# A two-layer fp32 network on one core: the recurrent layer's output projection as seven block products, plain rows at the start of the second MLP, and the first means further back

## The chip, the cores and the metric

The kernel runs on one core of one Trainium2 chip. The metric is the device time of one execution in microseconds (us). Three runs of the kernel before gave 2066.32, 2066.69 and 2067.29 us; the median is **2066.69 us**. PE is TensorE's matrix multiplication, PEld its weight load, DVE is VectorE, ACT ScalarE, POOL GpSimd, SP SyncE, which issues nearly all DMAs.

## What is computed

Two layers over 1024 tokens of 1024 features, all in fp32: layer 0 mixes tokens with a sliding-window attention, layer 1 with a gated recurrence; each is followed by an MLP, and a norm ends it. Cut to what matters here:

```python
def hgrn2_recurrence(h, lower_bound, w_in, g_norm, w_o):
    q, f, i, g = jnp.split(h @ w_in, 4, axis=-1)
    ...                                   # chunked gated recurrence, 8 heads of 128
    o = rmsnorm(o, g_norm) * jax.nn.silu(g.astype(jnp.float32))
    return o.astype(h.dtype) @ w_o        # 1024 x 1024: the output projection

def sqrelu_mlp(h, w_up, w_down):
    return jnp.square(jax.nn.relu(h @ w_up)) @ w_down

def reference(x, ...):
    for layer in range(2):
        h = rmsnorm(x, mix_norm[layer])
        y = attention(h, ...) if layer == 0 else hgrn2_recurrence(h, ...)
        x = x + y
        x = x + sqrelu_mlp(rmsnorm(x, mlp_norm[layer]), w_up[layer], w_down[layer])
    return rmsnorm(x, final_norm)
```

## The kernel before

**Tiles.** Activations lie transposed, features on the 128 partitions and tokens along the row: the residual stream is 8 feature tiles (`kt`) by 2 token halves (`hf`) of 128 x 512. Every fp32 operand is split into a high part (a cast to fp32r, mostly on ACT) and a low part (the difference, mostly on DVE); `split` (L523) does it for activations, `weight_split` (L505) for weights. A block product is then three matmuls, high by high, high by low, low by high (`mm3`, L487), each with 128x128 weights and a row of 512, or of 256 in the inner products. In a row of the profile `wh` and `wl` are split weights, `wr` a raw weight, `a` and `t` long- and short-lived tiles, `m` a few more, `sm` small ones, `d` DRAM, and `p` and `q` PSUM banks, four of each. Every operation is issued by one helper, so the line is L429 nearly everywhere.

**Order of work.** The program is first recorded as a list of operations in the order in which the code is written. A list scheduler (`Schedule`, L156) then lays each engine's queue out, with modelled costs, by the rank of an operation: its place in the list minus a `lead` that the code may set (`LEAD`, 100 places, for weights; `EVACUATE` for what reads a `p` bank). Nothing is reordered at run time: each engine goes through its queue, and an instruction that waits holds up all behind it on its engine.

**First means.** `scaled` (L589) makes the attention's input x times gain, split, and sums the squares over the 8 feature tiles on ACT and DVE. `token_rstd` (L546) then multiplies that sum by a constant column on PE (8 matmuls of one column) to get each token's mean and makes its normaliser.

**Recurrence and its output projection.** `hgrn` (L1631) runs 8 heads; head e+1's gates (projections) are interleaved with head e's `recurrence` (L1458), which ends with the head's gated output `g` for each half, split in two. `hgrn_out` (L1607), called once for each half, is a plain product: for each of 8 output blocks m one `p` bank gets 8 block products, is multiplied by the normaliser `r` and added to x. Between the two halves, `mlp_first` (L681) makes the second MLP's first operands: x times gain, split (`begin`, L631), and with `weigh(0)` (L625) the means of half 0, which also writes that half of x to DRAM.

**MLPs.** `mlp` (L918) computes the up product by a Strassen scheme of seven products over (feature halves) x (token halves), one pair of output rows at a time: `pair(m)` (L819) for m = 0 to 15. Products 1 and 2 of the rows 0 and 1 are begun early (`pair_first`, L805, called by `mlp_second`, L686). From row pair 2 on (`leaves`) the products 2, 3 and 4 aren't multiplied in full: two row pairs together compute each by a second Strassen level (`inner_products`, L779), seven quarter products with rows of 256, whose sums DVE adds up. `inner_operands` (L732) makes their operands. `weigh(1)` comes before the pairs.

The functions that the change touches, and what calls them:

Of the kernel before, what the change touches and what calls it, by code (L numbers as in the profile page):

```python
# [14 lines left out]
ALU = mybir.AluOpType  # L15
AX = mybir.AxisListType

P = 128
T = 1024
D = 1024  # L20
KT = D // P
NH = 2
TH = T // NH
# [351 lines left out]
class Net:  # L375
# [38 lines left out]
    def a(self, dt=F32, shape=(P, TH)):  # L414
        return self.tile("a", BUFS["a"], shape, dt)
# [185 lines left out]
    def square_relu(self, m, hf, c, psum):  # L601
# [79 lines left out]
    def mlp_first(self, layer):  # L681
        self.layer, self.hid, self.y = layer, {}, {}
        yield from self.begin(2 + layer)
        self.weigh(0)

    def mlp_second(self):  # L686
        self.first = [self.pair_first(m) for m in range(2)]
# [131 lines left out]
    def pair(self, m, x, leaves):  # L819
# [5 lines left out]
        up, half = self.io["up"][self.layer], MT // 2  # L825
        last, odd = m == half - 1, m % 2
        inner, four = [], ("12", "56", "73", "4")
        if leaves and odd:
            inner.append((2, (up[m - 1][:, TH:], 2), four, (1, 3, 5, 7)))
# [3 lines left out]
        elif leaves and m > 3:  # L833
            inner.append((4, (up[m - 2 + half][:, TH:], up[m - 1 + half][:, TH:]), four, (1, 3, 5, 7)))
            inner.append((3, (), four[2:], (2, 5)))
        w = self.strassen_weights(up[m], up[m + half], (2, 3, 4) if leaves else (1, 2), inner)

        def read(ps):
            z = self.t()
            self.copy(z, ps)  # L840
            return z
# [4 lines left out]
        def between(k):  # L846
            for z in now[k]:
                next(z)

        main, side = self.psum("q") if leaves else self.first[m], self.psum("q")  # L850
        now = [()] * 4
        if leaves:
            self.product(main, w[1], x[1], True)
            u1 = read(main)
            self.sums[2].append((m, u1))
            if odd:
                z2 = leaf(2, ((1, 2), (6, 5), (7, 3), (4,)))
                now = [[z2], [z2], [z2], [z2]]
            elif m > 3:
                z4, z3 = leaf(4, ((1, 2), (6, 5), (7, 3), (4,))), self.rest  # L860
                z3.send(w)
                now = [[z4, z3], [z4, z3], [z4], [z4]]
        between(0)
        self.product(side, w[5], x[5], True)
        p5 = read(side)
# [33 lines left out]
        if odd:  # L899
            for n, u in self.sums[2][-2:]:  # L900
                self.square_relu(n, 0, u, False)
        elif m > 3:
# [15 lines left out]
    def mlp(self, cut):  # L918

        x = self.mlp_second()  # L920
        for m in range(MT // 2):
            if m == 2:
# [535 lines left out]
    def recurrence(self, e, gates, totals, out):  # L1458
# [80 lines left out]
        for hf, (q, k) in enumerate(zip(qs, ks)):  # L1539
# [32 lines left out]
                totals.append(self.a())  # L1572
                self.ts("Pool", totals[hf], sq, 1.0, None, ALU.mult)
            self.stt(g, o, self.gain(5, e), g, ALU.mult, ALU.mult)
            keep = e < KT - 1
            y = self.split(g, self.t if keep else None)
            out[hf].append(self.put_by(y) if keep else y)
            yield

    def back(self, kept):  # L1580
# [23 lines left out]
            self.tt("DVE", new[hf], tv[:, :, 0], tv[:, :, 1], ALU.mult, n)  # L1604
        return at + n, new, *out

    def hgrn_out(self, hf, y, total):  # L1607
        r = self.t()
        self.copy(r, self.rstd(total, 0.25, 0.25))
        for m in range(KT):  # L1610
            w = self.blocks(self.weight(self.io["wg"][m]))
            x = self.t()
            self.dma(x, self.x[m][hf], 4 * P * TH)
            ps = self.psum()
            for kt in range(KT):
                self.mm3(ps, w[kt], y[kt], kt == 0, kt == KT - 1)
            z = self.t()
            self.tt("DVE", z, ps, r, ALU.mult)
            self.x[m][hf] = self.a()
            self.tt("any", self.x[m][hf], x, z, ALU.add)  # L1620

    def spill(self, hf):
        for kt in range(KT):
# [7 lines left out]
    def hgrn(self, layer):  # L1631
        self.hgrn_constants()
        x, r = self.finish(layer, True), [self.a() for _ in range(NH)]
        begun = [self.two_first(which, 0, x) for which in ((0, 3), (1, 2))]
        self.rs.append(self.token_rstd(self.sum_squares([self.x[kt][1] for kt in range(KT)]), keep=True))
        for y, z in zip(r, self.rs):
            self.copy(y, self.spread(z))
        self.spill(1)
        ys, totals = [[], []], []
        before = iter(())  # L1640
        for e in range(KT):
            got = []
            interleave(self.gates(e, x, self.rs, r, got, [None] * 2 if e else begun), before, 14, 13)
            before = self.recurrence(e, got, totals, ys)
# [31 lines left out]
def run(pieces):  # L1676
    for _ in pieces:
        pass
# [22 lines left out]
def layout(i):  # L1701
# [23 lines left out]
        "wg": f(i["hgrn_w_o"][0].reshape(KT, P, KT, P).transpose(2, 1, 0, 3).reshape(KT, P, D)),  # L1725
# [40 lines left out]
```

## Time and profile before

| | before |
|---|---|
| median of three runs | 2066.69 us |
| the profiled execution's own time | 2068.61 us |
| its span, first to last instruction | 2066.8 us |
| PE, matmuls | 2057.5 us busy, 12248 matmuls |
| DVE | 1831.0 us busy |
| ACT | 1203.6 us busy |
| DMA | 407.43 MB, mean 197 GB/s |
| granted TensorE clock, mean | .999 |

Matmuls overlap: the "mean ns" of one matmul is longer than the step from one start to the next. The step is read from the chain of waits instead, where a row that says `x183` is so many matmuls one behind the other with nothing between. The span leaves out 1.8 us of the execution's own time, and the profiled execution is 1.92 us over the median of the three runs.

### The profile page before, as it was taken

What the parts mean: (1) busy time and instruction counts of PE and PEld (TensorE: products, weight loads), DVE (VectorE), ACT (ScalarE), POOL (GpSimd) and SP (SyncE); (2) the same over time, 40 slices, a digit from 0 to 9 for tenths busy, and PEclk for the clock granted to TensorE, in tenths of its full rate; (3) what the DMA queues carried; (4) which work ended last, traced back from release to release, by engine and by line L of the source; (5) the groups of instructions that cost most, each with busy time, mean ns of one, the idle gap of its engine ahead of it and who ended that gap; (6) DMA issues with size and microseconds to landing.
All of it is one profiled execution on the core that took longest, in us unless ns stands there. A gap on an engine that the chain in (4) does not pass through costs nothing.

```text
span 2066.8 us, 35765 instructions
## 1 busy us (share of the span) xinstructions
PE 2057.5 (100%) x12248; PEld 1747.5 (85%) x12248; DVE 1831.0 (89%) x3696; ACT 1203.6 (58%) x2468; POOL 54.7 (3%) x121
## 2 busy tenths in 40 slices
PE   9999999999999999999999999999999999999998
PEld 7878788898898888888888888888888888888888
DVE  8899889999899979889988888887999989986985
ACT  7577887644565444666555555555765456544473
POOL 3020000000000000000000000000000000000000
PEclk9999999999999999999999999999999999999999
DMA  6212477877679977541322222677887768986822
GB/s 220 82 49 80 128 237 257 278 244 237 225 253 304 332 222 257 196 138 67 113 102 95 96 103 103 219 239 226 273 275 256 230 229 265 311 315 210 270 67 82
DMA packets 225750, 407.43 MB, mean 197 GB/s; under 512 B 25232, under 2 KB 30352, under 8 KB 225568
## 3 DMA queue, kind: packets, MB, share of 16 engines
q1 hardware_dynamic: 225536, 405.12, 59.3%
q8 instruction: 96, 1.57, 0.3%
q14 instruction: 86, 0.70, 0.1%
q10 hardware_dynamic: 32, 0.03, 0.0%
HBM read 321.17 MB, written 83.89 MB: 196 GB/s over the span
## 4 chain that ended last, share of the span: by engine, by line
PE 96%; issue 1%; DVE 1%; ACT 0%; DMA 0%; POOL 0%; POOLq 0%; SPq 0%; DVEq 0%; ACTq 0%
PE p L429 51%; PE q L429 45%; DVE a L429 1%; DMA a<-in_x 0%; DVE m L429 0%; DVE t L429 0%; DVE wl L429 0%; ACT t L429 0%; ACT a L429 0%; DVE sm L429 0%; ACT wh L429 0%; POOL a L429 0%; POOLq L1740 0%; SPq L429 0%; ACT m L429 0%
## 5 line engine op out<-in xcount | busy, mean ns | idle before, releaser
L429 PE MATMUL p<-a,wh 128*128 128x512 f32 (+1 forms) x2880 | 805.0, 364 | 0.0
L429 PE MATMUL q<-a,wh 128*128 128x512 f32 x2112 | 652.9, 390 | 0.0
L429 PEld LDWEIGHTS p<-a,wh 128*128 128x128 f32 x2880 | 515.2, 189 | 84.4 <-issue 0.4
L429 PE MATMUL p<-a,wl 128*128 128x512 f32 (+1 forms) x1440 | 520.5, 362 | 0.0
L429 PEld LDWEIGHTS q<-a,wh 128*128 128x128 f32 x2112 | 389.7, 188 | 75.5
L429 PE MATMUL q<-a,wl 128*128 128x512 f32 x1056 | 410.2, 389 | 0.0
L429 ACT CAST wh<-m 128x512 fp32r<-128x512 f32 (+1 forms) x338 | 206.3, 613 | 262.1 <-PE q L429 172.2
L429 ACT CAST wh<-wr 128x512 fp32r<-128x512 f32 (+1 forms) x351 | 210.9, 603 | 227.8 <-PE p L429 165.2
L429 PEld LDWEIGHTS p<-a,wl 128*128 128x128 f32 x1440 | 271.6, 189 | 40.3 <-DVE wl L429 0.2
L429 DVE TENSOR_TENSOR wl<-m,wh 128x512 fp32r<-128x512 f32 (+1 forms) x338 | 226.8, 676 | 52.1 <-ACT wh L429 47.4
L429 DVE TENSOR_TENSOR wl<-wr,wh 128x512 fp32r<-128x512 f32 x352 | 233.2, 666 | 35.6 <-ACT wh L429 34.6
L429 PEld LDWEIGHTS q<-a,wl 128*128 128x128 f32 x1056 | 198.3, 188 | 41.9
L429 DVE TENSOR_TENSOR a<-t,a 128x512 fp32r<-128x512 f32 (+2 forms) x314 | 207.1, 679 | 14.5 <-PE q L429 8.8
L429 DVE TENSOR_TENSOR t<-t,t 128x512 f32<-128x512 f32 (+3 forms) x337 | 196.7, 602 | 13.8 <-ACT t L429 8.2
L429 ACT CAST a<-t 128x512 fp32r<-128x512 f32 (+1 forms) x234 | 139.1, 610 | 31.7 <-DMA t<-d 10.5
L429 ACT ACTIVATE t<-t 128x512 f32<-128x512 f32 x180 | 113.3, 632 | 73.4 <-DVE t L429 70.3
L429 ACT COPY t<-q 128x512 f32<-128x512 f32 (+2 forms) x201 | 111.3, 558 | 28.8 <-PE q L429 23.3
L429 PE MATMUL p<-wh,a 128*128 128x512 f32 x384 | 125.7, 397 | 0.0
L429 DVE TENSOR_TENSOR m<-wr,wr 128x512 f32<-128x512 f32 (+1 forms) x188 | 121.6, 647 | 2.9 <-DMA wr<-in_down 1.6
L429 DVE TENSOR_TENSOR t<-t,p 128x256 f32<-128x256 f32 x294 | 119.7, 416 | 3.7 <-PE p L429 1.8
L429 PEld LDWEIGHTS q<-t,t 128*64 128x64 f32 (+1 forms) x2160 | 96.0, 144 | 12.1 <-issue 8.1
L429 PE MATMUL q<-t,t 128*64 128x32 f32 (+2 forms) x2160 | 104.7, 229 | 0.0
(129 smaller groups left out, 2327.4 us busy)
## 6 DMA issues: line engine op xcount, KB each, us to landing
t<-d SPq DMA_DIRECT2D x548, 256.0 KB, 4.2
d<-t SPq DMA_DIRECT2D x244, 256.0 KB, 3.2
wr<-in_down SPq DMA_DIRECT2D x224, 256.0 KB, 4.2
wr<-in_up SPq DMA_DIRECT2D x178, 256.0 KB, 3.8
wr<-in_win SPq DMA_DIRECT2D x68, 256.0 KB, 2.8
a<-d SPq DMA_DIRECT2D x60, 256.0 KB, 3.7
wr<-in_wqkv SPq DMA_DIRECT2D x48, 256.0 KB, 2.9
d<-a SPq DMA_DIRECT2D x48, 256.0 KB, 3.9
```

The lines of the kernel that those rows point to most:

```text
L429: fn(*[place(a) for a in args], **{k: place(v) for k, v in kw.items()})
```

## The change

1. **Output projection in seven products.** The 1024 x 1024 product of both token halves is computed together as a Strassen scheme over 2 x 2 blocks: input features in two halves (`HK` = 4 tiles each), output features in two halves, tokens in two halves. The products run in the order 1, 5, 2, 6, 3, 7, 4; each is 4 x 4 block products of three matmuls. Their activation operands (1: half 0's first four heads; 2: half 0's last four; 5, 6, 4, 7: differences; 3: half 1's last four) are made in `recurrence` by a new `out_operands`, their weight operands by a new `out_weight`.
2. **Sums begun in PSUM banks.** Four `p` banks hold 1, then 1+5, then 1+5+6, then all of 1+5+6+7. Four `q` banks start from a value that ACT or DVE writes into the bank: first a matmul writes the bank ("mark"), ACT copies product 1's sum over it, and product 2's matmuls go on adding; likewise before product 3 (a copy of 1+5+6) and product 4 (a difference on DVE).
3. **Second MLP.** Row pairs 2 and 3 of layer 1 are plain products; inner products begin at row pair 4 (`INNER`). `weigh(0)` and `weigh(1)` of layer 1 come behind row pair 1. `begin`'s steps are taken four at a time, behind product 2 and behind product 4 of the projection.
4. **First means later.** The one-column matmuls of the attention's first means (half 0) get a lead of -120 (`BEHIND`).

The helper's line is now L433. The diff, cut to its core:

```diff
+BEHIND = 120
+INNER = 2, 4
+FIRSTS = 2, 2
+ORDER, AHEAD, HELD = (1, 5, 2, 6, 3, 7, 4), 2, (3, 7, 4)
...
-        return h, self.token_rstd(self.sum_squares([self.x[kt][hf] for kt in range(KT)]))
+        total = self.sum_squares([self.x[kt][hf] for kt in range(KT)])
+        self.s.lead = 0 if hf else -BEHIND
+        r = self.token_rstd(total)
+        self.s.lead = 0
+        return h, r
...
     def mlp_first(self, layer):
         yield from self.begin(2 + layer)
-        self.weigh(0)
+        if not layer:
+            self.weigh(0)
...
-        self.weigh(1)
+        if not self.layer:
+            self.weigh(1)
...
+        elif not begun:
+            own = self.psum()
+            self.product(main, w[1], x[1], True)
+            u1 = read(main)
+            self.product(own, w[2], x[2], True)
+            self.tt("DVE", u1, own, u1, ALU.add)
+            self.square_relu(m, 0, u1, False)
...
-            self.pair(m, x, m > 1)
+            self.pair(m, x, m >= INNER[self.layer])
+            if self.layer and m == 1:
+                self.weigh(0)
+                self.weigh(1)
...
-            keep = e < KT - 1
-            y = self.split(g, self.t if keep else None)
-            out[hf].append(self.put_by(y) if keep else y)
+            self.out_operands(e, hf, g, out)
...
+    def out_operands(self, e, hf, g, x):
+        p, last = e % HK, e == KT - 1
+        def put(name, z):
+            y = self.split(z, self.a if last else self.t)
+            x[name].append(y if last else self.put_by(y))
+        if hf == 0:
+            put(1 if e < HK else 2, g)
+            self.beside = g
+        elif e < HK:
+            self.tt("any", self.beside, g, self.beside, ALU.subtract)
+            put(5, self.beside)
+            self.later.append((self.keep(self.beside), self.keep(g)))
+        else:
+            t, q = (self.back(z) for z in self.later[p])
+            self.tt("any", t, g, t, ALU.subtract)
+            put(6, t)
+            self.tt("any", self.beside, self.beside, t, ALU.subtract)
+            put(4, self.beside)
+            self.tt("any", q, g, q, ALU.subtract)
+            put(7, q)
+            put(3, g)
...
+        def scaled_sum(hf, m, z):
+            u, out = self.t(tag="m"), self.a()
+            self.tt("DVE", u, z, r[hf], ALU.mult)
+            self.dma(out, self.x[m][hf], 4 * P * TH)
+            self.tt("any", out, u, out, ALU.add)
+            self.x[m][hf] = out
...
+        products(1, main, True)
+        for m in range(HK):
+            self.copy(p1[m], main[m])
+        products(5, main, False)
+        for m in range(HK):
+            w, z = ready[2, 0]
+            self.mm(side[m], w[0][:, :P], z[0], True, True)
+            self.copy(side[m], p1[m], psum=False)
+            self.tt("DVE", p5[m], main[m], p1[m], ALU.subtract)
+        products(2, side, False)
+        for m in range(HK):
+            scaled_sum(0, m, side[m])
+        yield
+        products(6, main, False)
+        for m in range(HK):
+            self.copy(side[m], main[m])
+        products(3, side, False)
+        for m in range(HK):
+            scaled_sum(1, m, side[m])
+        products(7, main, False)
+        for m in range(HK):
+            self.tt("DVE", side[m], main[m], p5[m], ALU.subtract)
+            scaled_sum(1, m + HK, main[m])
+        products(4, side, False)
+        for m in range(HK):
+            scaled_sum(0, m + HK, side[m])
+        yield
...
-        for y in ys:
-            y[:-1] = [self.take_back(kept) for kept in y[:-1]]
-        self.hgrn_out(0, ys[0], totals[0])
-        run(self.mlp_first(layer))
-        self.hgrn_out(1, ys[1], totals[1])
+        first = self.mlp_first(layer)
+        for _ in self.hgrn_out(y, totals):
+            for _ in range(HK):
+                next(first)
+        run(first)
```

What it moves, at three places of PE's queue. A row names the bank that is written, then the two operands, with their buffer numbers. The first place is the attention's first projection, where the first means (`q` from `c` and the sum `t_234`) stand. Before:

```order
L429 MATMUL p_263<-wh_294,a_319 128x512
L429 MATMUL p_272<-wh_294,a_300 128x512
L429 MATMUL q_400<-c_69,t_234 128x1 x4
L429 MATMUL p_272<-wl_310,a_300 128x512
L429 MATMUL p_272<-wh_294,a_319 128x512
L429 MATMUL p_243<-wh_337,a_322 128x512
```

and PE's same place in the changed kernel:

```order
L433 MATMUL p_253<-wh_339,a_353 128x512
L433 MATMUL p_253<-wl_360,a_353 128x512
L433 MATMUL q_466<-c_69,t_234 128x1
L433 MATMUL p_253<-wh_339,a_382 128x512
L433 MATMUL q_466<-c_69,t_234 128x1
L433 MATMUL p_263<-wh_339,a_353 128x512
L433 MATMUL q_466<-c_69,t_234 128x1
```

The means' first matmul stood behind 46 large matmuls, inside the fourth feature tile; now it stands behind 65, inside the sixth (`a_353`), and the four of one kind are taken one by one between large ones.

The second place is the output projection on PE. Before, one bank gets one output block, all features in a row:

```order
L429 MATMUL p_16672<-a_15900,wh_16468 128x512
L429 MATMUL p_16672<-a_15908,wh_16468 128x512
L429 MATMUL p_16672<-a_15900,wl_16486 128x512
L429 MATMUL p_16672<-a_15920,wh_16468 128x512
L429 MATMUL p_16672<-a_15935,wh_16468 128x512
```

and the changed kernel's PE between product 5 (bank `p_16333` is its last) and product 2 (banks `q_16909` to `q_16918`):

```order
L433 MATMUL p_16333<-a_16279,wl_16609 128x512
L433 MATMUL q_16909<-a_16508,wh_16466 128x512
L433 MATMUL q_16913<-a_16508,wh_16466 128x512
L433 MATMUL q_16915<-a_16508,wh_16466 128x512
L433 MATMUL q_16918<-a_16508,wh_16466 128x512
L433 MATMUL p_16293<-a_16525,wh_16907 128x512
L433 MATMUL p_16293<-a_16534,wh_16907 128x512
L433 MATMUL q_16909<-a_16508,wh_16466 128x512
L433 MATMUL q_16909<-a_16545,wh_16466 128x512
L433 MATMUL q_16909<-a_16508,wl_16664 128x512
```

The four marks stand between the products, and the scheduler put two matmuls of product 6 (bank `p_16293`) ahead of product 2's first, which goes on adding in the bank that the mark has written. Over the whole projection the 384 large matmuls of before have become 340, the marks among them.

The third place is PE's hand-over to the second MLP. In the changed kernel product 4's last matmuls (bank `q_16918`) are followed by those of a row pair of the MLP (banks `q_17505`, `p_17538`):

```order
L433 MATMUL q_16918<-a_17095,a_17269 128x512
L433 MATMUL q_16918<-a_17024,a_17298 128x512
L433 MATMUL q_17505<-a_17073,wh_17039 128x512
L433 MATMUL q_17505<-a_17104,wh_17039 128x512
...
L433 MATMUL q_17505<-a_17121,wl_17048 128x512
L433 MATMUL p_17538<-a_17527,wh_17060 128x512
L433 MATMUL q_17543<-a_17073,wh_17136 128x512
```

Bank `q_17505` needs only what product 2 gave. `p_17538` is the first that needs the sums of product 4 (`a_17527` is the high part of x times gain for the first of them); from there on matmuls into it are taken between those into `q_17543`. Where the plain rows 2 and 3 stand in place of inner products, the up product of the second MLP has 72 large matmuls more and 126 of 256 columns fewer.

More of the change, by code (lines that the diff above doesn't have):

```diff
@@ L827, in pair @@
         inner, four = [], ("12", "56", "73", "4")
+        if leaves and odd and m >= FIRSTS[self.layer]:
+            inner.append((2, (up[m - 1][:, TH:], 2), four, (1, 3, 5, 7)))
         if leaves and odd:
-            inner.append((2, (up[m - 1][:, TH:], 2), four, (1, 3, 5, 7)))
             inner.append((3, (self.fourth, 3), four if last else four[:2], (6, 9, 10, 11)))
@@ L848, in between @@
                 next(z)
-        main, side = self.psum("q") if leaves else self.first[m], self.psum("q")
+        begun = m < FIRSTS[self.layer]
+        main = self.first[m] if begun else self.psum("q")
+        side = self.psum() if m < FIRSTS[self.layer] - 2 else self.psum("q")
         now = [()] * 4
         if leaves:
[L853 to L856, printed above, removed]
+            if not begun:
+                self.product(main, w[1], x[1], True)
+                u1 = read(main)
+                self.sums[2].append((m, u1))
+            if odd and not begun:
                 z2 = leaf(2, ((1, 2), (6, 5), (7, 3), (4,)))
                 now = [[z2], [z2], [z2], [z2]]
-            elif m > 3:
+            elif m > INNER[self.layer] + 1:
                 z4, z3 = leaf(4, ((1, 2), (6, 5), (7, 3), (4,))), self.rest
@@ L1605, in double @@
         return at + n, new, *out
[L1607 to L1620, printed above, removed]
+    def out_operands(self, e, hf, g, x):
[19 more added lines that the diff above has]
+            put(3, g)
@@ new lines, in hgrn_out, with operand, products @@
+    def hgrn_out(self, x, totals):
+        kept, y, r = {}, {}, [self.a() for _ in range(NH)]
+        order = [(name, p) for name in ORDER for p in range(HK)]
+        ready = {}
+        def operand(name, p):
+            w = self.out_weight(name, p, kept)
+            z = x[name][p]
+            return w, self.take_back(z) if isinstance(z, list) else z
+        def products(name, bank, start, apart=False):
+            todo = order.index((name, 0))
+            for p in range(HK):
+                for q in order[: todo + p + 1 + AHEAD]:
+                    if q not in ready:
+                        ready[q] = operand(*q)
+            got = [ready[name, p] for p in range(HK)]
+            turns = [(p, m) for p in range(HK) for m in range(HK)]
+            more = {} if start else {"skip_group_check": True}
+            for p, m in sorted(turns, key=lambda k: k[1]) if apart else turns:
+                c, (w, z) = slice(m * P, m * P + P), got[p]
+                self.mm3(bank[m], (w[0][:, c], w[1][:, c]), z, start and p == 0, p == HK - 1, **more)
+        def scaled_sum(hf, m, z):
[4 more added lines that the diff above has]
+            self.x[m][hf] = out
+        for hf in range(NH):
+            self.copy(r[hf], self.rstd(totals[hf], 0.25, 0.25))
+        main, side = [self.psum() for _ in range(HK)], [self.psum("q") for _ in range(HK)]
+        p1, p5 = ([self.a() for _ in range(HK)] for _ in range(2))
+        products(1, main, True)
[25 more added lines that the diff above has]
+        yield
@@ L1638, in hgrn @@
         self.spill(1)
-        ys, totals = [[], []], []
+        y, totals, self.later = {k: [] for k in range(1, 8)}, [], []
         before = iter(())
```

42 lines of the change are left out of this document (34 added, 8 removed).

## The prediction

> **What bounds the kernel now.** I read the page's busy times first, then the chain that ended last, then its rows in order of time.
>
> ```profile
> span 2066.8 us, 35765 instructions
> PE 2057.5 (100%) x12248; PEld 1747.5 (85%) x12248; DVE 1831.0 (89%) x3696; ACT 1203.6 (58%) x2468; POOL 54.7 (3%) x121
> PE 96%; issue 1%; DVE 1%; ACT 0%; DMA 0%; POOL 0%; POOLq 0%; SPq 0%; DVEq 0%; ACTq 0%
> ```
>
> PE is busy throughout, and 96% of the chain is PE. So time changes in two ways: by matmuls that PE has more or fewer, each worth its step, and by places where PE stands or is slowed. The steps come from chain rows (start, duration, engine, bank, count), one matmul right behind the other:
>
> ```profile
> 1404.70 41.62 PE p L429 x183
> ...
> 1500.52 2.75 PE q L429 x12
> 1507.45 2.87 PE p L429 x24
> ```
>
> The first and the second are of 512 columns: 41.62/183 = .2274 us (2.75/12 = .229). The third is of 256: 2.87/24 = .1196 us.
>
> DVE, 89% busy, is the engine that could become the bound. Its load by stage stands in windows (length, then busy us of PE, PEld, DVE, ACT, POOL with counts, granted clock, DMA share, GB/s): one head of the recurrence, then its end, the old projection in two windows, the hand-over to the MLP, and its first row pairs.
>
> ```profile
> 1135.00:1189.00 54.00, 54.00 (x470) 45.69 (x469) 47.03 (x106) 29.59 (x64) 0.61 (x2) 1.00 0.28 100
> 1340.00:1372.00 32.00, 32.00 (x361) 27.90 (x360) 25.38 (x65) 17.38 (x43) 0.61 (x2) 1.00 0.68 228
> 1372.00:1400.00 28.00, 28.00 (x126) 23.19 (x125) 23.70 (x37) 18.56 (x33) 0.00 (x0) 1.00 0.83 278
> 1400.00:1447.00 47.00, 47.00 (x221) 39.31 (x220) 36.82 (x67) 25.11 (x44) 0.00 (x0) 1.00 0.69 217
> 1447.00:1470.00 23.00, 23.00 (x106) 18.97 (x106) 22.96 (x40) 16.29 (x30) 0.00 (x0) 1.00 0.79 255
> 1470.00:1500.00 30.00, 30.00 (x139) 24.98 (x137) 29.48 (x63) 22.71 (x43) 0.00 (x0) 1.00 0.83 287
> ```
>
> In the fifth window DVE has 22.96 of 23 us and PE still starts 106 matmuls (23/.2274 = 101). A full DVE alone does not hold PE up.
>
> **The matmuls, -8.7 us.** The projection has 2 x 8 x 8 x 3 = 384 large matmuls. Seven products of 4 x 4 blocks make 7 x 16 x 3 = 336, and four marks make 340: 44 fewer, 44 x .2274 = -10.01 us. In the second MLP, row pairs 2 and 3 each get the products 2, 3 and 4 in full: 2 x 3 x 12 = 72 large, +16.37 us. Their three sets of seven quarter products go, 3 x 7 x 6 = 126 of 256 columns: -15.07 us. Together **-8.71 us**. That these counts are what is issued the order of the changed program shows, so "the change does not do it" is no rival here. `weigh` moved behind row pair 1 brings no matmul, only DVE and ACT work and stores.
>
> **The start, -2.9 us.** At the first means (start, duration, engine, operation; in brackets the idle time before it and who ended it), with windows beside:
>
> ```profile
> 16.45 0.61 PE L429 MATMUL p<-wh,a 128*128 128x512 f32 x2
> 18.09 1.05 PE L429 MATMUL q<-c,t 128*128 128x1 f32 x8 [1.03 <-DVE t L429]
> ...
> 17.34 0.69 DVE L429 TENSOR_TENSOR t<-t,t 128x512 f32<-128x512 f32 x1
> 20.71 0.74 DVE L429 SCALAR_TENSOR_TENSOR a<-a,c,a 128x512 fp32r<-128x512 f32 x1
> ```
> ```profile
> 17.00:19.00 2.00, 0.97 (x9) 0.91 (x9) 2.00 (x6) 2.00 (x4) 0.00 (x0) 1.00 0.51 173
> 19.00:21.00 2.00, 2.00 (x8) 1.64 (x8) 1.97 (x11) 0.93 (x4) 0.00 (x0) 0.69 0.77 180
> 21.00:23.00 2.00, 2.00 (x6) 1.53 (x5) 2.00 (x11) 0.00 (x0) 0.00 (x0) 0.50 0.79 246
> 23.00:25.00 2.00, 2.00 (x9) 1.61 (x9) 0.82 (x3) 0.89 (x2) 0.00 (x0) 0.96 0.85 210
> ```
>
> Behind the two matmuls from 16.45 the next could start at 16.45 + 2 x .2274 = 16.90. It starts at 18.09, when DVE's sum is there: 1.19 us lost. Then the granted clock falls to .69, .50 and .96, which loses 2 x (.31 + .50 + .04) = 1.70 us. With the means behind 65 large matmuls in place of 46, 19 more (4.3 us) stand ahead of them, and the sum is ready by 18.1. I take the clock drop to follow from the wait, since it begins right behind it and nowhere else in the quoted windows: **-2.89 us**. The new cover is the feature tiles kt 4 and 5, whose operands must be there: the row at 20.71 is kt 6's low part and ends at 21.45, while at full clock PE begins kt 6 at 16.90 + 26 x .2274 = 22.8. So I see no wait in its place.
>
> [...]
>
> The moved means also make the normaliser later, and with it the reading of the four banks:
>
> ```profile
> 24.09 0.62 ACT L429 CAST wh<-wr 128x512 fp32r<-128x512 f32 x1 [3.62 <-PE p L429]
> 24.73 1.28 ACT L429 ACT_TABLE_LOAD   x1
> ...
> 26.88 0.16 DVE L429 SCALAR_TENSOR_TENSOR sm<-sm,sm 128x4 f32<-128x4 f32 x1
> 27.06 1.89 DVE L429 TENSOR_TENSOR wl<-wr,wh 128x512 fp32r<-128x512 f32 x3
> 30.54 0.48 DVE L429 SCALAR_TENSOR_TENSOR t<-p,sm,a 128x256 f32<-128x256 f32 x1
> ```
>
> The normaliser ends at 27.04, 8.0 us behind the means (18.09 + .97), but 3.62 us of that is ACT waiting for PE in the cast ahead of it in its queue. The banks are read at 30.54; with PE 2.9 us earlier that is wanted at 27.6. The means now run from 16.90 + 19 x .2274 = 21.2 to about 22.3, and the normaliser ends 8.0 - 3.6 = 4.4 us (26.7) to 8.0 us (30.3) behind. So 0 to +2.7 us; I take 0, since ACT's wait was for a matmul that now comes earlier.
>
> **New work on DVE and ACT, +.7 us.** A DVE instruction of 512 takes (1.89 - .69)/2 = .60 us a step, from the x3 row above and the single one at 17.34. Heads 4 to 7 get four subtractions and three splits' low parts more each: 7 x .60 = 4.2 us, so 51.2 of 54 us in the first window's kind of head. PE hides it as long as DVE is under the head's length; if none were hidden, 4 x 4.2 = 16.8 us. I take .5, near the full DVE window, which lost nothing. In the projection DVE has 18 instructions between reading product 3's banks and product 7's, 18 x .60 = 10.8 us, against one product's 48 x .2274 = 10.9 us, and the same again up to product 4's: no slack. Overall 127 DVE instructions, 77 us, lie beside 368 matmuls, 83.7 us.
>
> Begun sums cost a wait at three places. The nearest rows for a write or read of a bank:
>
> ```profile
> L429 ACT CAST wh<-wr 128x512 fp32r<-128x512 f32 (+1 forms) x351 | 210.9, 603 | 227.8 <-PE p L429 165.2
> L429 ACT COPY t<-q 128x512 f32<-128x512 f32 (+2 forms) x201 | 111.3, 558 | 28.8 <-PE q L429 23.3
> ```
>
> A seed takes .56 to .60 us behind its mark, and four marks with two matmuls of product 6 cover 6 x .2274 = 1.36 us. Queued behind it on PE stands all of product 2. Bounds: 0, and 2 us (four copies, 4 x .56 = 2.2, with only the first mark beside them); I take .2, near the first copy, which the cover hides. Products 3 and 4 have a whole product as cover for their seeds; I take 0, bound above by rival 2.
>
> [...] No run here shows a seeded bank yet. [...]
>
> **Hand-over to the MLP, +.3.** After product 4's last matmul the last bank's sum goes through DVE (times r, .69, then the addition, with two others' ahead of it, .60 each), ACT (x times gain, the row below), a cast and its low part, which PE needs.
>
> ```profile
> 11.77 0.72 ACT L429 ACTIVATE a<-a,c 128x512 fp32r<-128x512 f32 x1
> ```
>
> That is .69 + 3 x .60 + .72 + .60 + .69 = 4.5 us and five changes of engine, whose cost no row shows by itself. Between that last matmul and the first that needs this low part the changed order has 30 large matmuls that need nothing of it, 6.8 us, which leaves 2.3 us for the five. Bounds 0 to 2 us; I take .3.
>
> **DMA, +.5.** The projection's stage needs 113 transfers of 256 KB, 29.6 MB. PE's work between their first uses is 317 large matmuls, 72.1 us, and the last head's small ones:
>
> ```profile
> 1341.98:1370.61 28.63, 17.27 (x67) 11.98 (x67) 0.00 (x0) 0.00 (x0) 1.00 0.69 231
> 10.00:15.00 5.00, 5.00 (x24) 4.13 (x23) 4.79 (x9) 5.00 (x10) 0.00 (x0) 1.00 1.06 393
> DMA packets 17965, 32.59 MB, mean 251 GB/s; under 512 B 1994, under 2 KB 2250, under 8 KB 17952
> ```
>
> The first row has 67 large matmuls of the `p` banks in 28.63 us: 28.63 - 67 x .2274 = 13.4 us of others. So 86 us, or 98 with some 12 us of early issue: 302 to 344 GB/s. The stage's mean from 1320 to 1450 was 251; the start of the program moved 393. I take +.5 within 0 to 2, near 393, because 251 was what was asked for, not a limit.
>
> **Sum.** -8.71 - 2.89 + .5 + .2 + .3 + .5 = -10.1. The profiled execution's own 2068.61 becomes 2058.5. It stands 1.92 us above the median of the three runs, 2066.69; with that taken off, **2056.6 us**.
>
> **Rival 1: the start gives less.** The drop of the clock comes from something else, or a later wait takes its place. For it: 1.03 us idle against a drop of about 4 us, and the normaliser's bound of +2.7. Against it: the clock is 1.00 in all windows quoted that don't follow the wait. If 1.70 stays: 2058.3; with a late normaliser too, 2061.
>
> **Rival 2: DVE becomes the bound** between products. For it: 10.8 of 10.9 us, twice. Against it: the window with DVE full. If it comes four instructions (2.4 us) late at products 7 and 4, that is +4.8, and with the hand-over's 2 us +6.8: 2061.4 to 2063.4.
>
> **Rival 3, slower: weights arrive late in the projection.** At 251 GB/s, 29.6 MB take 118 us against 98: +20 us, 2076. It decides from the rate at which 29.6 MB take 98 us, 302 GB/s; it is slower than before below about 265. For it: the mean of 251. Against it: 393 at the start, with transfers of the same kind.
>
> **How the numbers follow.** Forecast .63 (own range 2054.8 to 2058.2), rival 1 .18, rival 2 .12, rival 3 .07. Low end: no allowance needed (-1.5) and one timed spread (2067.29 - 2066.32 = 1.0) less: 2054.0. High end: into rival 2, 2063.0. What a measurement of this kernel can tell from no change is about 0.2%, 4.1 us: faster ends at 2062.6, slower begins at 2070.8. Forecast, rival 1 and half of rival 2 are faster, .88; half of rival 2 and the milder rival 3 are within, .07; the rest is slower, .05.
>
> **What the profile after would show.** PE has 12248 + 28 - 126 = 12150 matmuls. The bracket at the first means is gone and the clock in 19:23 is 1.00 (else rival 1); the first read of a `p` bank with `sm` comes at 27 to 28. In the projection PE's rows show no brackets over .3 us on ACT `q` or DVE `q` (else rival 2), nor on DMA (rival 3, with GB/s under 302). I am wrong if PE stands over 5 us in the recurrence's second half, which I hold hidden.

## The result and the profile after

| | before | changed |
|---|---|---|
| median | 2066.78 us (8 runs, 2066.32 to 2068.11) | **2060.80 us** (8 runs, 2058.19 to 2065.49) |
| ratio | | **.9971, 95% interval .9962 to .9980** |
| the traced execution | 2068.61, span 2066.8 | 2058.19, span 2056.3 |

The medians differ by 6.0 us, the two traces by 10.4. The trace of before was of one of its longer executions, that of the changed kernel of one of its shortest; over all 19 executions of the changed kernel in this study the median is 2060.77. Most of what follows comes from that gap: the first pair of traces alone would have confirmed the sum of the prediction to .3 us, by luck of which executions were traced.

The page of the changed kernel:

```profile
span 2056.3 us, 35559 instructions
PE 2046.4 (100%) x12150; PEld 1735.8 (84%) x12150; DVE 1845.8 (90%) x3699; ACT 1222.7 (59%) x2500; POOL 59.2 (3%) x121
...
PE 95%; DVE 2%; issue 1%; DMA 0%; ACT 0%; POOL 0%; POOLq 0%; DVEq 0%; ACTq 0%
```

12150 matmuls, as counted; PE still carries the chain. At the first means (windows first, then rows of PE, then of DVE):

```profile
17.00:19.00 2.00, 2.00 (x10) 1.69 (x9) 2.00 (x12) 1.96 (x6) 0.00 (x0) 1.00 0.84 250
19.00:21.00 2.00, 2.00 (x10) 1.65 (x9) 1.97 (x10) 0.84 (x2) 0.00 (x0) 1.00 0.73 206
21.00:23.00 2.00, 2.00 (x15) 1.80 (x14) 1.34 (x8) 1.12 (x2) 0.00 (x0) 1.00 0.89 276
```
```profile
21.07 0.28 PE L433 MATMUL q<-c,t 128*128 128x1 f32 x2
21.21 0.48 PE L433 MATMUL p<-wh,a 128*128 128x512 f32 x1
```
```profile
25.09 0.16 DVE L433 SCALAR_TENSOR_TENSOR sm<-sm,sm 128x4 f32<-128x4 f32 x1
27.20 0.48 DVE L433 SCALAR_TENSOR_TENSOR t<-p,sm,a 128x256 f32<-128x256 f32 x1 [0.47 <-PE p L433]
```

The bracket behind which PE stood is gone, the clock is 1.00, and the first read of a bank at 27.20 waits for PE, not for the normaliser, which ended at 25.25 (25.09 + .16). The means start at 21.07 (worked out before: 21.2).

The projection's products in the chain (start, duration, engine, bank, count):

```profile
1378.90 10.88 PE q L433 x48
1389.78 10.43 PE p L433 x46
1400.20 10.88 PE q L433 x48
1411.09 10.88 PE p L433 x48
1421.96 13.61 PE q L433 x60
```

Product 2 (1378.90) to product 4 and the first twelve matmuls of the MLP (1421.96) follow one another with nothing between; 10.88/48 = .2267 us a step. Neither a seed nor the hand-over made PE wait in this trace. The stretch behind it, in windows:

```profile
1440.00:1445.00 5.00, 5.00 (x23) 4.10 (x23) 5.00 (x9) 3.92 (x7) 0.00 (x0) 1.00 0.92 280
1445.00:1450.00 5.00, 5.00 (x24) 4.14 (x23) 4.58 (x9) 3.47 (x7) 0.00 (x0) 1.00 0.87 297
1450.00:1455.00 5.00, 5.00 (x24) 4.14 (x23) 5.00 (x9) 5.00 (x11) 0.00 (x0) 1.00 0.63 229
1455.00:1460.00 5.00, 5.00 (x23) 3.81 (x22) 5.00 (x10) 5.00 (x11) 0.00 (x0) 1.00 0.31 105
```

From 1450 DVE and ACT are both busy without a gap, and PE still has its 22 matmuls in 5 us. DVE and ACT have no slack left there; the experiments show how narrow that is.

### The profile page after: what moved, and what is told of

It is laid out like the page before. It is cut to its first block, busy times and chain, and to the rows that moved or that the text cites. A ratio compares the mean times of both kernels' runs of the same rounds, so it can differ in the third digit from the quotient of the medians.

```text
span 2056.3 us, 35559 instructions
## 1 busy us (share of the span) xinstructions
PE 2046.4 (100%) x12150; PEld 1735.8 (84%) x12150; DVE 1845.8 (90%) x3699; ACT 1222.7 (59%) x2500; POOL 59.2 (3%) x121
## 4 chain that ended last, share of the span: by engine, by line
PE 95%; DVE 2%; issue 1%; DMA 0%; ACT 0%; POOL 0%; POOLq 0%; DVEq 0%; ACTq 0%
PE p L433 49%; PE q L433 46%; DVE t L433 1%; DVE a L433 0%; DVE m L433 0%; DVE wl L433 0%; DMA d<-t 0%; DVE sm L433 0%; POOL a L433 0%; ACT m L433 0%; POOLq L1861 0%; ACT t L433 0%; DVEq L433 0%; POOLq L433 0%; ACTq L433 0%
## 5 line engine op out<-in xcount | busy, mean ns | idle before, releaser
L433 PE MATMUL p<-a,wh 128*128 128x512 f32 (+1 forms) x2680 | 751.9, 364 | 0.0
L433 PE MATMUL q<-a,wh 128*128 128x512 f32 x2180 | 673.8, 390 | 0.1
L433 PEld LDWEIGHTS p<-a,wh 128*128 128x128 f32 x2680 | 479.2, 189 | 78.5 <-DVE a L433 0.6
L433 PE MATMUL p<-a,wl 128*128 128x512 f32 (+1 forms) x1340 | 484.7, 362 | 0.0
L433 PEld LDWEIGHTS q<-a,wh 128*128 128x128 f32 x2180 | 402.7, 188 | 79.5 <-ACT t L433 0.5
L433 PE MATMUL q<-a,wl 128*128 128x512 f32 x1088 | 423.0, 389 | 0.0
L433 ACT CAST wh<-m 128x512 fp32r<-128x512 f32 (+1 forms) x336 | 205.3, 612 | 252.4 <-PE q L433 155.9
L433 ACT CAST wh<-wr 128x512 fp32r<-128x512 f32 (+1 forms) x323 | 194.6, 604 | 189.2 <-PE p L433 123.0
L433 PEld LDWEIGHTS p<-a,wl 128*128 128x128 f32 x1340 | 252.7, 189 | 37.2 <-DVE wl L433 0.4
L433 DVE TENSOR_TENSOR wl<-m,wh 128x512 fp32r<-128x512 f32 (+1 forms) x336 | 225.4, 676 | 55.4 <-ACT wh L433 51.1
L433 PEld LDWEIGHTS q<-a,wl 128*128 128x128 f32 x1088 | 204.3, 188 | 43.3 <-DVE wl L433 0.3
L433 DVE TENSOR_TENSOR wl<-wr,wh 128x512 fp32r<-128x512 f32 (+1 forms) x324 | 214.4, 665 | 21.3 <-ACT wh L433 19.0
L433 DVE TENSOR_TENSOR t<-t,t 128x512 f32<-128x512 f32 (+3 forms) x360 | 211.1, 607 | 15.1 <-ACT t L433 8.5
L433 DVE TENSOR_TENSOR a<-t,a 128x512 fp32r<-128x512 f32 (+1 forms) x317 | 209.1, 677 | 12.5 <-PE q L433 8.3
L433 ACT CAST a<-t 128x512 fp32r<-128x512 f32 (+1 forms) x237 | 141.6, 611 | 33.1 <-DVE t L433 10.6
L433 ACT ACTIVATE t<-t 128x512 f32<-128x512 f32 x196 | 123.6, 632 | 61.6 <-DVE t L433 58.1
L433 PE MATMUL p<-wh,a 128*128 128x512 f32 x384 | 124.8, 395 | 0.0
L433 DVE TENSOR_TENSOR m<-wr,wr 128x512 f32<-128x512 f32 (+1 forms) x186 | 120.3, 648 | 4.4 <-DMA wr<-in_down 3.1
L433 ACT COPY t<-q 128x512 f32<-128x512 f32 (+1 forms) x199 | 109.9, 558 | 23.2 <-PE q L433 11.5
L433 DVE TENSOR_TENSOR t<-t,p 128x256 f32<-128x256 f32 x273 | 111.3, 416 | 5.9 <-PE p L433 3.2
L433 ACT CAST a<-a 128x512 fp32r<-128x512 f32 x136 | 83.1, 620 | 49.5 <-DVE a L433 40.5
L433 DVE TENSOR_TENSOR a<-a,a 128x512 fp32r<-128x512 f32 (+2 forms) x151 | 101.0, 680 | 11.2 <-PE p L433 5.0
```

What stands on the lines that cost most here:

```text
L433: fn(*[place(a) for a in args], **{k: place(v) for k, v in kw.items()})
```

## The experiments

All ratios are to the kernel before, run on the same chip in the same series.

**The changed kernel again, twice** (no edit).

> The changed kernel once more, unchanged, for a second trace. Theory A: the terms of the sum are right (matmuls -8.7, start -2.9) and the -6.0 us between the medians is smaller than the -10.5 us between the two traces because the changed kernel waits somewhere in most executions and did not in the traced one: median 2059.5 to 2061.5 again, and a trace whose span is 2 to 3 us over 2056.3 shows PE's extra idle in one place. Rival B: the traces are what executions usually are and the first series of times was high: median 2057 to 2058.5. Rival C: what differs is spread thinly over the whole span, with no place of its own: a trace over 2058 us has the same steps, each a little longer.

> The changed kernel a third time, unchanged. The two traces so far were of 2058.19 and 2059.32, below the median of its 13 timed executions, 2060.2. Theory A: the longer executions have single waits of .6 to 1.5 us behind transfers that land late, at changing places (as the one of .64 at 695 us in the second trace, and two of 1.0 and 1.5 us in the first MLP of the kernel with the projection alone): median 2059.5 to 2061, and the trace's excess over 2058.2 is such waits. Rival B: they lose it in the stretch from 1440 to 1480 us, where DVE is full: waits there.

Medians 2059.57 (5 runs, ratio .9965, .9951 to .9978) and 2060.93 (6 runs, .9969, .9957 to .9981). The two traces were of executions of 2059.32 and 2060.77, the last at the median of all 19. The span of the first, 2057.5, is 1.2 us over 2056.3, not the 2 to 3 of Theory A; most of it lies in the first MLP. Where PE stands in the trace of the second, the third of the changed kernel (in brackets the idle time and who ended it):

```profile
396.40 0.73 PE L433 MATMUL q<-a,wh 128*128 128x512 f32 x2 [0.58 <-ACT t L433]
```
```profile
581.71 0.58 ACT L433 COPY t<-q 128x512 f32<-128x512 f32 x1 [0.84 <-DMA d<-t]
582.33 0.69 DVE L433 TENSOR_TENSOR t<-t,t 128x512 f32<-128x512 f32 x1 [0.40 <-ACT t L433]
582.35 0.30 PEld L433 LDWEIGHTS q<-a,wh 128*128 128x128 f32 x2 [0.69 <-ACT t L433]
582.35 0.73 PE L433 MATMUL q<-a,wh 128*128 128x512 f32 x2 [0.48 <-ACT t L433]
```
```profile
697.16 0.73 PE L433 MATMUL q<-a,wh 128*128 128x512 f32 x2 [0.63 <-ACT a L433]
```
```profile
1365.46 0.65 PE L433 MATMUL q<-c,t 128*128 128x128 f32 x4 [1.31 <-DVE t L433]
```

Three are in the first MLP, which the change does not name. The one at 582 shows its mechanism whole: ACT wants to copy a bank into a `t` tile whose earlier contents are still on their way to DRAM (`d<-t`); the copy starts .84 us late, and PE, which needs the bank, .48. The same row of ACT waits .22 us in the first trace, where PE had that much in hand:

```profile
580.59 0.59 ACT L433 COPY t<-q 128x512 f32<-128x512 f32 x1 [0.22 <-DMA d<-t]
```

The wait at 396 goes back to a late transfer too, a weight load for which DVE waits 1.83 us in this trace and .8 in the first:

```profile
391.67 0.42 DVE L433 TENSOR_TENSOR m<-m,wr 128x256 f32<-128x256 f32 x1 [1.83 <-DMA wr<-in_up]
```

The waits at 697 and 1365 don't: there PE waits behind a DVE that works without a gap. So Theory A of the second run, single waits behind late transfers, holds for two of the four; its Rival B does not hold: no wait of PE over .06 us stands between 1440 and 1480. What each stage adds over PE's bare steps (for every pair of successive matmuls, the time from start to start less the step of its shape, summed), in us:

| stage (own time of each trace) | before, second trace (2066.56) | changed, first (2058.19) | changed, third (2060.77) |
|---|---|---|---|
| start, 0 to 30 | 3.5 | 2.4 | 2.2 |
| attention, 30 to 340 | 6.5 | 5.8 | 5.7 |
| first MLP and after, 340 to 930 | .0 | .1 | **2.6** |
| recurrence, 930 to 1345 | 7.5 | 7.6 | 7.6 |
| its last head's end, 1345 to 1385 | 1.1 | 2.2 | **3.2** |
| projection, hand-over, 1385 to 1480 | -.1 | .4 | .2 |
| the rest | 1.6 | 1.8 | 1.4 |

From the first to the last column, both of typical executions, with the differences taken before rounding: -8.71 (matmuls) - 1.3 - .7 + 2.5 + .1 + 2.1 + .3 - .2 = -5.9; the times differ by 2060.77 - 2066.56 = -5.8.

**The kernel before again.**

> The kernel before once more, unchanged, for a second trace of its start. If the wait of 1.19 us and the clock drop of 1.70 us are in every execution, this trace has both within 0.2 us. If the first trace was one of the longer executions (2068.61 against a median of 2067), this one is 1 to 2 us shorter and the difference is in the first 25 us: no drop, or no wait.

Median 2066.77, traced at 2066.56. The wait is there, shorter, and the clock does not drop:

```profile
17.78 1.05 PE L429 MATMUL q<-c,t 128*128 128x1 f32 x8 [0.67 <-DVE t L429]
```
```profile
19.00:21.00 2.00, 2.00 (x10) 1.64 (x9) 1.97 (x11) 0.73 (x2) 0.00 (x0) 1.00 0.87 197
21.00:23.00 2.00, 2.00 (x11) 1.65 (x10) 2.00 (x12) 0.79 (x2) 0.00 (x0) 1.00 0.82 244
```

So the 1.70 us of half clock, more than half of the start's term, is in the execution that the prediction read and not in this typical one. What the start adds to PE's bare steps is 5.5 us in the first trace and 3.5 in this one: the 2.0 us between the two spans.

**The start alone**, an edit of `scaled` in the kernel before.

```diff
+BEHIND = 120
...
+        total = self.sum_squares([self.x[kt][hf] for kt in range(KT)])
+        self.s.lead = 0 if hf else -BEHIND
+        r = self.token_rstd(total)
...
```

> The kernel before with the first means' lead of -120 alone. If the wait causes the clock drop, as the prediction has it: -2.9 us against before (2063.8), clock 1.00 from 17 to 25 us. If the drop has another cause: -1.2 us (2065.5) and a drop of the clock somewhere else in the first 40 us. If the start as traced is not what timed executions do: within 0.5 us of before.

2065.88 against 2067.18 of before: -1.3 us, ratio .9995 (.9986 to 1.0003). The medians fit "the wait alone" (-1.2); the interval reaches from -2.9 to +.6, so it does not exclude the full -2.9 nor nothing. The clock is 1.00 at 17 to 25, and no drop came elsewhere.

**The changed kernel without the moved means.**

```diff
-BEHIND = 120
+BEHIND = 0
```

> The changed kernel with the lead back at 0. If the start gives 2.9 us in every execution: 2.9 us over the changed kernel, some 2063.5 against its 2060.8, and the clock drop is back at 19 to 23 us. If the start's part is smaller in timed executions: 0 to 1.2 us over it.

2060.90 us, .9970 (.9959 to .9981): .1 us over the 19 executions' 2060.77, 1.3 over the five of its own series (2059.57). The smaller part is right, and these runs can't tell it from nothing. Its trace has no drop, and no wait at the means either:

```profile
7.32 0.63 PE L433 MATMUL p<-wl,a 128*128 128x512 f32 x1
7.74 1.05 PE L433 MATMUL p<-wh,a 128*128 128x512 f32 x2
17.24 0.95 PE L433 MATMUL q<-c,t 128*128 128x1 f32 x8
```

The clock becomes full only at 9.02 us here. Until then PE's large matmuls start .42 us apart or more (7.32 to 7.74), so PE comes to the means later, when the sum is there. The projection alone (below) has the same: full clock at 8.36, no wait. In eleven of the fourteen traces the clock is full between 4.2 and 6.5 us. There PE's 100th large matmul starts at 30.8 us with the wait (two traces without a drop) and at 29.5 to 30.0 with the means moved. The one trace with moved means and a late full clock, at 8.50 (`weigh` early, below), starts it at 31.05, the projection alone at 31.03. So the moved means bring that matmul .8 to 1.3 us forward in the traces whose clock is full early, and not in those where it is late (31.05 against 31.03). That is a reading of traces; no run set that time.

**The projection alone**: the changed kernel with the start's and the MLP's parts undone (`weigh` too stands where it was, for both layers).

```diff
-INNER = 2, 4
+INNER = 2, 2
-BEHIND = 120
+BEHIND = 0
...
-        if not layer:
-            self.weigh(0)
+        self.weigh(0)
...
-        if not self.layer:
-            self.weigh(1)
+        self.weigh(1)
...
-            if self.layer and m == 1:
-                self.weigh(0)
-                self.weigh(1)
```

> The projection in seven products alone: inner products from row pair 2, the means of the second MLP where they were, first means where they were. By matmuls alone -10.0 us against before (2056.8). If DVE holds PE up in the first row pairs, whose inner products then lie behind the projection: 2 to 8 us less of a gain (2059 to 2065), with PE idle behind DVE between the projection and row pair 4. If what costs the changed kernel its extra time in most executions is in the projection, this one shows it too: a spread of over 2 us between its runs.

2065.22 us, .9992 (.9983 to 1.0001). Of -10.0 us only 2.0 arrive, and the interval reaches from -3.5 to +.2. Its trace, of an execution of 2066.88, has PE's matmuls as counted, and this between projection and MLP:

```profile
1457.74 0.74 PE L433 MATMUL q<-a,wh 128*128 128x512 f32 x2 [2.22 <-ACT t L433]
1466.11 0.73 PE L433 MATMUL q<-a,wh 128*128 128x512 f32 x2 [0.55 <-ACT t L433]
```
```profile
1455.00:1460.00 5.00, 2.78 (x10) 1.91 (x10) 5.00 (x9) 5.00 (x11) 0.00 (x0) 0.90 0.60 218
1460.00:1465.00 5.00, 5.00 (x19) 3.97 (x18) 5.00 (x10) 2.63 (x5) 0.00 (x0) 0.76 0.95 320
```

DVE and, up to 1460, ACT are full, PE stands, and half clock follows the wait: 5 x .10 + 5 x .24 = 1.7 us lost, 3.4 us at half. From 1440 to 1480 this trace adds 6.4 us to PE's bare steps; 3.0 more lie in the first MLP.

**Inner products from row pair 2 again, means kept late.**

```diff
-INNER = 2, 4
+INNER = 2, 2
```

> The changed kernel with inner products from row pair 2 in the second MLP (72 large matmuls fewer, 126 of 256 columns more, -1.3 us of PE), its means still behind row pair 1. Theory A, the plain rows keep DVE and ACT free behind the projection: PE waits there again, 2062 to 2065, with the waits between 1445 and 1475 us. Rival B, the later means do that: 2058.5 to 2059.5, no wait over 0.5 us there.

2067.03 us, ratio 1.0000 (.9991 to 1.0009): 6.3 us slower than the changed kernel with 1.3 us less for PE to do. That is Theory A, at a time 2 us above its range. From 1440 to 1480 the trace adds 7.6 us:

```profile
1472.34 0.80 PE L433 MATMUL q<-a,wh 128*128 128x512 f32 x2 [3.29 <-ACT wh L433]
1474.36 0.79 PE L433 MATMUL q<-a,wl 128*128 128x512 f32 x1 [1.22 <-DVE wl L433]
```
```profile
1466.15 4.88 DVE t L433 x8
1471.04 0.60 DVE m L433
```
```profile
1471.67 0.62 ACT L433 CAST wh<-m 128x512 fp32r<-128x512 f32 x1 [1.79 <-DVE m L433]
```

The second piece is of its chain: eight DVE instructions of `t`, operands and sums, stand ahead of the one that makes the weight sum `m`; ACT waits 1.79 us for `m` to cast `wh` from it, and PE waits for `wh`.

**Means of the second MLP early again, plain rows kept.**

```diff
-        if not layer:
-            self.weigh(0)
+        self.weigh(0)
...
-        if not self.layer:
-            self.weigh(1)
+        self.weigh(1)
...
-            if self.layer and m == 1:
-                self.weigh(0)
-                self.weigh(1)
```

> The changed kernel with the second MLP's means (weigh) where they were, behind the first operands and ahead of the row pairs; plain rows kept. Theory A: 2059.5 to 2061.5, as the changed kernel. Rival B: 2063 to 2066, with PE waiting for ACT or DVE between 1445 and 1460 us.

2067.54 us, 1.0001 (.9993 to 1.0010): Theory A's time fails, and Rival B's wait is there, with a time 1.5 us above its range. From 1440 to 1480 the trace adds 8.0 us; ACT is the engine that is late, with 20 instructions begun in 10 us and no gap:

```profile
1453.36 1.22 PE L433 MATMUL q<-a,wh 128*128 128x512 f32 x2 [3.56 <-ACT t L433]
```
```profile
1450.00:1455.00 5.00, 1.64 (x4) 1.35 (x5) 5.00 (x9) 5.00 (x11) 0.00 (x0) 0.73 0.91 311
1455.00:1460.00 5.00, 4.84 (x14) 3.31 (x13) 5.00 (x10) 5.00 (x11) 0.00 (x0) 0.58 0.45 163
```

So each half of the MLP's change is needed; either one undone takes back the whole gain. One thing differs from the kernel before: with the projection in one piece `weigh(0)` comes behind all of it, and no longer between the two halves.

**The MLP's change alone**: the kernel before with `mlp_first`, `mlp_second`, `pair` and `mlp` of the changed one.

```diff
+INNER = 2, 4
+FIRSTS = 2, 2
...
```

> The kernel before with the plain rows and the later means in the second MLP, and nothing else. By matmuls +1.3 us (2068.3 to 2068.7). If the plain rows help by themselves, with the old projection too: 2065 to 2067. Together with the run of the projection alone it says whether the two parts add up: -2.0 and this one against -6 to -7 for all of it.

2067.38 us against 2066.79, 1.0003 (.9995 to 1.0012): +.6, between the matmuls' +1.3 and nothing, and the interval holds both. It is in neither expected range. That the plain rows help by themselves is not shown; no wait of PE stood there before. The parts do not add up: -2.0, +.6 and the start's -1.3 make -2.7 apart, and -6.0 together.

**Sums added on DVE in place of begun in banks**, for product 2 as shown and for products 3 and 4 in the same way.

```diff
+            if seed is not None:
+                self.tt("DVE", seed, z, seed, ALU.add)
+                z = seed
...
-            w, z = ready[2, 0]
-            self.mm(side[m], w[0][:, :P], z[0], True, True)
-            self.copy(side[m], p1[m], psum=False)
...
-        products(2, side, False)
+        products(2, side, True)
         for m in range(HK):
-            scaled_sum(0, m, side[m])
+            scaled_sum(0, m, side[m], p1[m])
```

> The changed kernel with no sum begun in a bank: products 2, 3 and 4 start from nothing, the four marks are gone, and DVE adds the twelve earlier sums after reading the banks. Matmuls: 4 x .2274 = -.9 us. If DVE has room: 2059 to 2060. Theory A, DVE is full from product 7 to the first row pairs and 12 more instructions (12 x .60 = 7.2 us) delay the hand-over: 2062 to 2067, with PE waiting between 1445 and 1470 us.

2065.44 us, .9991 (.9982 to .9999): +4.7 us though PE has four matmuls fewer. PE waits at 1450.34 (.81, ACT), 1452.09 (.42, DVE) and 1453.89 (1.07, DVE), half clock follows for 3.4 us (granted .99 and .67 in the windows 1450 to 1455 and 1455 to 1460: 5 x .01 + 5 x .33 = 1.7 us lost), and 1440 to 1480 adds 5.4 us. Theory A holds.

**Two more plain row pairs.**

```diff
-INNER = 2, 4
+INNER = 2, 6
```

> The changed kernel with two more plain row pairs: inner products of the second MLP from row pair 6. Matmuls +1.3 us. Theory A, nothing waits behind the projection any more: +1.3 us, 2061 to 2062. Rival B, the longer executions still lose 1 to 3 us where DVE is full and the relief ends that: 2058.5 to 2060.

2060.76 us (6 runs, .9970, .9959 to .9982). The +1.3 us does not show, and no gain either; a spread of 2058.65 to 2062.90 hides which. This stays open.

**One more `t` tile, one `m` fewer.**

```diff
-BUFS = {"a": 60, "t": 18, "m": 6, ...
+BUFS = {"a": 60, "t": 19, "m": 5, ...
```

> The changed kernel with 19 short-lived tiles t in place of 18 and 5 of m in place of 6. If the single waits behind late stores of t tiles make up the longer executions: 1 us less, 2058.5 to 2059.5, and fewer waits of over .5 us in the MLPs. If m is what the projection's sums need: PE waits behind DVE m in the projection, 2061 to 2064.

2059.79 us (6 runs, .9968, .9956 to .9979): 1.0 us under the changed kernel's 2060.77, which these intervals can't tell from nothing. `m` was not missed. Its one trace has single waits of .37 and .28 us in the MLPs (694.90 and 1819.86 us) and none over .5 there, so such waits became fewer in this trace. The changed kernel itself had a median of 2059.57 in one series, so this kernel is not shown to be better.

## Why the prediction was right or wrong

The time, 2060.8, lies inside 2054.0 to 2063.0; faster was right, by less than the forecast: -6.0 where -10.1 was summed, and outside the likeliest case's own range (2054.8 to 2058.2). That the time lies inside the range is in part luck: the high end was set by rival 2, and the loss came from the start and the first MLP. Between typical traces, -5.9 differs from -10.1 by 4.2 us. The start gained 1.6 less than summed; the first MLP cost 2.5 and the recurrence with its end 1.7 more. Against that stand .7 of the attention, .7 of seeds, hand-over and DMA, and .2 of the rest, which came out better. (In the chances, .63 + .18 + half of .12 is .87, not .88.)

- **Matmuls, -8.71: right.** 12150 as counted, steps unchanged.
- **The start, -2.89: the first term that was off**, and by size. "I take the clock drop to follow from the wait" made a lasting term out of one execution's 1.70 us. Two further traces with the wait (.67 us in the kernel before, 1.06 with the MLP's change alone) have no drop. The sum also took the drop off twice: the 1.92 us by which the traced execution stood above the median is the same drop and the longer wait (the two traces of before differ by 2.0 us, and so do their starts). What is left is the wait, -1.3 between the two typical traces and between the medians of the start alone, and nothing in the traces whose clock is full late (8.36 to 9.02 us; 31.05 against 31.03 at the 100th large matmul). Rival 1, "the start gives less" (.18), had the size; neither of its reasons came: no trace with the means moved has a drop at the start, and the normaliser was not late.
- **New work on DVE in the recurrence, +.5: mis-sized.** The load came as worked out: 51.70 us of 54 in the last full head, worked out 51.2.

```profile
1291.00:1345.00 54.00, 54.00 (x470) 45.60 (x469) 51.70 (x117) 29.78 (x64) 0.93 (x4) 1.00 0.69 238
```

  The heads hide it. The end of the last does not: PE waits at 1362 to 1365 for DVE's `t`, and ahead of it on DVE stand the projection's low parts (`wl`) and weight sums (`a` from `m` and `wr`), here in the typical trace:

```profile
1362.85 1.28 DVE L433 TENSOR_TENSOR wl<-a,wh 128x512 fp32r<-128x512 f32 x2
1364.38 0.68 DVE L433 TENSOR_TENSOR a<-m,wr 128x512 f32<-128x512 f32 x1
1364.98 1.42 DVE L433 TENSOR_TENSOR t<-t,m 128x256 f32<-128x256 f32 x4
```

  The stage adds 1.1 us more than in the kernel before in the first trace and 2.1 in the typical one. The sign of being wrong, over 5 us in the recurrence's second half, did not come.
- **Seeds +.2, hand-over +.3, DMA +.5: no wait of PE came for any of them**, and the stage from 1385 to 1480 adds .3 to .5 us of the 1.0. What the begun sums are worth, 4.7 us, is only seen when DVE has to do the additions; 2059 to 2060 was expected of that run if DVE has room, and it has none: 5.00 of 5 us in each of the four windows from 1440 to 1460. On DMA the threshold of 302 GB/s was too high: the traced stage, 1360 to 1445, moved 267 on the mean, without a wait of PE for a transfer.
- **What the sum left out: +2.5 us in the first MLP.** I priced what the change names; the list scheduler laid out ACT's and SP's queues anew in stages that it doesn't name. There the changed kernel's traces have places with a few tenths of slack behind a weight load, a store or a full DVE (396, 582, 697), which cost PE 0, 1.3 and 2.5 us in three executions. The ten traces with the new projection have .0 to 3.0 us there, the four without it .0 to .1, though the code of that stage is the same in all. That the new layout is the cause is the reading of these traces; no run changed that layout by itself. The changed kernel without the moved means has .0 there in its one trace, so the moved means may have a part in it; that stays open.
- **The MLP's +1.30 (16.37 - 15.07) was counted as a cost only.** The plain rows and the later means are what lets the projection's -10 us through: the gain is 2.0 us with both undone and 0 with either one undone, and these three intervals overlap. Rival 2 had the mechanism (DVE as the bound, 2061.4 to 2063.4), but for the changed kernel, which avoids it between the products and at the hand-over.

The changed kernel's four marks cost PE 4 x .2274 = .9 us by the step; with the seeds added on DVE after reading in their place the kernel took 4.7 us longer, so in this kernel the measurement speaks for the marks. No run tried a third way.

## What to carry to other kernels

Read the stage that a removed or shortened piece of work hands over to: a PE-bound projection that is cut by 10 us gave back 8, 6.4 of them in its trace where the engines behind it are full, and paying 1.3 us of matmuls and moving the means later, to relieve those engines, let most of it through (-6.0 us in all). A loss seen in one traced execution is a term only if a second trace has it: take a second trace of the kernel before you enter a clock drop or a single wait in the sum, and don't take the same loss off again as the distance of that execution from the median. And where a scheduler lays out the whole program, a change in one stage may take the slack out of another.

## What the runs showed of the hardware

- **Half clock behind waits lasted 3.4 to 6.9 us in the five traces with a drop.** In the first trace of before it is 3.41 us, 19.74 to 23.16, at a granted clock of .50. In the others, where large matmuls begin .42 to .43 us apart for that time, it is worked out as twice what the windows lack of a clock of 1.00: 3.4 us with the projection alone, behind a wait of 2.22 us (.90 and .76 in 5 us each), and 3.4 with DVE's additions, behind .81, .42 and 1.07 us (.99 and .67); 6.8 us with inner products from row pair 2, behind 3.29 and 1.22 us (.66 in the 10 us from 1470), and 6.9 with the means early, behind 3.56 us (.73 and .58 in 5 us each).
- **The length of a wait alone did not tell whether the clock dropped.** At the first means 1.03 us (first trace of before) was followed by half clock; 1.06 us there with the MLP's change alone and .67 in the second trace of before were not, with 1.00 from 17 to 25 us in both. Nor was the 1.31 us at 1365 in the third trace of the changed kernel (1.00 from 1364 to 1367). What decides it was not shown.
- **DVE and ACT, both full, did not hold PE up in the changed kernel.** With both at 5.00 of 5 us PE lost nothing (1450 to 1460, 24 and 23 matmuls begun in 5 us each); with twelve DVE additions more the kernel took 4.7 us longer, and of the 5.4 us that its trace adds from 1440 to 1480, 1.7 is clock.
